# Turning the weights of the first 512 keys on the tensor engine in query blocks 8 to 15 of a forgetting-attention layer

## The chip, the cores and the metric

The kernel runs on one core of one Trainium2 chip. The metric is device time in microseconds (us), the median over runs. A core has TensorE (PE; its weight loads are listed as PEld), VectorE (DVE), ScalarE (ACT), GpSimd (POOL), a queue on SyncE (SP) that issues most DMAs, and 16 DMA engines. Each has its own list of instructions and goes through it in order.

## The reference

One layer, sequence 2048, width 1024, 16 heads of 64, all in float32: forgetting attention, then an MLP. `x` is (1, 2048, 1024).

```python
h = rms_norm(x, norm_mix) * (1 + sc_m) + sh_m
q, k, v, f_pre = split(h @ fox_w_in)
q = rms_norm(q, fox_q_norm); k = rms_norm(k, fox_k_norm)      # per head
F = cumsum(log_sigmoid(f_pre + fox_b_f))                      # per head, over time
logits = q @ k.T * 64 ** -0.5 + (F[t] - F[s])                 # only s <= t
x = x + g_m * ((softmax(logits) @ v) @ fox_w_out)
h = rms_norm(x, norm_mlp) * (1 + sc_f) + sh_f
x = x + g_f * (square(relu(h @ w_mlp_in)) @ w_mlp_out)
```

The shifts, scales and gates (`sc_m` and so on) come from `silu(c) @ w_ada + b_ada`.

## The kernel before

**Two halves.** Up to about 1500 us the kernel does the projections and the attention, from then on the output projection and the MLP. Products that need float32 accuracy are made from a high and a low part, three matmuls each (`mm3`, lines 132 to 134).

**Attention.** The 16 heads go in 8 pairs `g`; each pair goes through 16 query blocks `i` of 128 queries; each block through its two heads `h`. Block `i` sees `W = (i + 1) * 128` keys. For one (g, i, h):

- `att_scores`: TensorE makes the scores of up to 1024 keys into one of two PSUM tiles `S` (lines 537, 538; line 540 adds the mask); VectorE adds `F`, writes them to `L` (three buffers, float32, 2048 wide) and takes the maximum (line 544, line 549).
- `att_exp`: ScalarE does Exp in place on `L` (line 555) and then, in chunks of up to 1024 keys (`PW`), writes the weights times 32768 as f16 into the front half of a tile `ph` (line 562): the high part.
- `att_transpose`: VectorE writes the low part, `L * 32768 - high`, behind it (line 574). In the last pair, from block 8 on, GpSimd takes 256 columns of each chunk wider than 512 (lines 578, 579). Then the SP queue issues one DMA transpose of the chunk, both parts (line 582), into a tile `pT`, which holds keys on partitions. There are four `ph` and five `pT`.
- `att_values`: TensorE multiplies each turned block of 128 keys with the values, high part with high and low values side by side (line 600), low part with the high values (line 601), into `po`; after the second head VectorE and GpSimd finish the block (lines 608 to 611) and SP writes it to DRAM (line 613).

In the order of the code a head's scores come first, then the turning of the head before it, then its own Exp; the value products follow two to four heads later.

**Beside it** run the projections of the next head pair (`sweep`): `psq` matmuls (lines 487 to 489) on `hT` blocks that SP loads (`hl`, line 403) and ScalarE and GpSimd split (lines 406, 407); their results are normed, and q and k are turned by TensorE through `pqk` (lines 435, 445): four float32 transposes into one bank, read by ScalarE and VectorE (lines 437, 438, 447, 448). `pqk` sits in the pool `psT`, which has one bank:

```python
psT = st.enter_context(tc.tile_pool(name="psT", bufs=1, space=PSUM))
NL, NPH, NPT, NK, NV, NQD = 3, 4, 5, 6, 7, 1
AHEAD, LEAD, LAG_S, LAG_L = 1, 0.7, 3, 2
```

In the first pairs the rest of `w_ada` is read as well: `wa` tiles of 512 KB, summed on VectorE (lines 195, 197).

**Order.** The code interleaves attention and projections by shares of work done. A planner then fixes the order on each engine when the kernel is built: it goes by the order of the code and by its own estimates of when an operand and a buffer are ready, with score matmuls ahead (`PR_S = 100`, the other offsets are 0).

Of the kernel before, what the change touches and what calls it, by code (L numbers as in the profile page):

```python
# [14 lines left out]
F32 = mybir.dt.float32  # L15
# [3 lines left out]
AF = mybir.ActivationFunctionType  # L19
ALU = mybir.AluOpType  # L20
# [4 lines left out]
P = 128  # L25
# [4 lines left out]
HD = 64  # L30
KB = D // P
NT = S // P
TJ = 512
# [6 lines left out]
PSCALE = 32768.0  # L40
PW = 1024
# [4 lines left out]
PR_S, PR_T, PR_E, PR_PL, PR_PO, PR_OT = 100, 0, 0, 0, 0, 0  # L46
PR_Q, PR_QE, PR_SP, PR_SN, PR_AD, PR_DT = 0, 0, 0, 0, 0, 0
EPOOL, WOP = 0, 0
POOL_B, POOL_I, POOL_G = 2, 8, 7
NEARLY, EARLY0 = 5, 12  # L50
TAPER, LEAD1 = 6.6, 0.6
QSH, QDM = 0, 0
LEAD0, NORM_AT, ADA0, ADA1, NF = 0.5, 8, 60, 10, 5


# [2 lines left out]
def fox_layer(ctx, tc, x, c, norm_mix, norm_mlp, w_ada, b_ada, w_mlp_in, w_mlp_out,  # L58
              fox_w_in, fox_b_f, fox_q_norm, fox_k_norm, fox_w_out, out):
    nc = tc.nc  # L60
# [18 lines left out]
    ident = con.tile([P, P], F32, name="ident")  # L79
# [56 lines left out]
    def pri(n):  # L136
        return tc.high_priority(offset=n)
# [3 lines left out]
    blk = blk8[:RB]  # L141
# [25 lines left out]
    pt = psQ.tile([P, TJ], F32, tag="Q", name="ptrows")  # L167
# [7 lines left out]
    with ExitStack() as st:  # L175
        psS = st.enter_context(tc.tile_pool(name="psS", bufs=2, space=PSUM))
        psT = st.enter_context(tc.tile_pool(name="psT", bufs=1, space=PSUM))
# [4 lines left out]
        def big(nm):  # L182
# [4 lines left out]
                                       op0=ALU.mult, op1=ALU.mult)  # L187
# [334 lines left out]
        def att_scores(g, i, h, st, L):  # L522

            j, rb = divmod(i, RB)
            W = (i + 1) * P
            q, qz = qT[g, j]
            qs = slice(rb * P, (rb + 1) * P)
            mx = sb.tile([P, NJ // 2], F32, tag="mx", name=f"mx{g}_{i}_{h}", bufs=6)
            for cch in range(j + 1):
                w = min(TJ, W - cch * TJ)  # L530
                k = kT[g, cch]
# [16 lines left out]
            with pri(PR_T):  # L548
                nc.vector.tensor_reduce(out=st[:, h:h + 1], in_=mx[:, :j // 2 + 1], axis=AX.X, op=ALU.max, negate=True)  # L549

        def att_exp(g, i, h, st, L):

            W = (i + 1) * P
            with pri(PR_E):
                nc.scalar.activation(L[:, :W], L[:, :W], AF.Exp, bias=st[:, h:h + 1], scale=1.0,  # L555
                                     accum_out=st[:, 2 + h:3 + h])
            phs = []
            for s0 in range(0, W, PW):
                w = min(PW, W - s0)
                ph = sb.tile([P, 2 * PW], F16, tag="ph", name=f"ph{g}_{i}_{h}_{s0}", bufs=NPH)  # L560
                with pri(PR_E):
                    nc.scalar.activation(ph[:, :w], L[:, s0:s0 + w], AF.Copy, scale=PSCALE)  # L562
                phs.append(ph)
            return phs

        def att_transpose(g, i, h, L, phs):
            W = (i + 1) * P
            pts = []
            for n, ph in enumerate(phs):
                s0 = n * PW  # L570
                w = min(PW, W - s0)
                c = w - min(w, POOL_B * P) if i >= POOL_I and g >= POOL_G and w > TJ else w
                with pri(PR_PL):
                    nc.vector.scalar_tensor_tensor(ph[:, w:w + c], L[:, s0:s0 + c], PSCALE, ph[:, :c],  # L574
                                                   op0=ALU.mult, op1=ALU.subtract)
                    if c < w:
                        lt = L[:, s0 + c:s0 + w]
                        nc.gpsimd.tensor_scalar(lt, lt, PSCALE, None, op0=ALU.mult)
                        nc.gpsimd.tensor_tensor(ph[:, w + c:2 * w], lt, ph[:, c:w], op=ALU.subtract)
                pT = sb.tile([P, 2 * PW // P, P], F16, tag="pT", name=f"pT{g}_{i}_{h}_{s0}", bufs=NPT)  # L580
                with pri(PR_DT):
                    nc.sync.dma_start_transpose(pT[:, :2 * w // P, :], ph[:, :2 * w])
                pts.append(pT)
            return pts

        po_of, n_po = {}, [0]
        po_all = psO.tile([P, 2, 2, P], F32, tag="O", name="po")
# [1 line left out]
        def att_values(g, i, h, st, pts):  # L589
            nb = i + 1  # L590
            if h == 0:
                po_of[g, i] = po_all[:, n_po[0] % 2]
                n_po[0] += 1
            po = po_of[g, i]
            for b in range(nb):
                v = vT[g, b // RB][:, b % RB, h, :]
                pT, bb = pts[b * P // PW], b % (PW // P)
                nw = min(PW // P, nb - b + bb)
                with pri(PR_PO):
                    nc.tensor.matmul(po[:, h, :], lhsT=pT[:, bb, :], rhs=v, start=(b == 0), stop=False)  # L600
                    nc.tensor.matmul(po[:, h, 0:HD], lhsT=pT[:, nw + bb, :], rhs=v[:, 0:HD],
                                     start=False, stop=(b == nb - 1))
                if b % RB == RB - 1:
                    yield
            if h == 1:
                ot = sb.tile([P, 2, HD], F32, tag="ot", name=f"ot{g}_{i}", bufs=2)
                with pri(PR_OT):
                    nc.vector.reciprocal(st[:, 4:6], st[:, 2:4])
                    nc.vector.tensor_reduce(out=ot, in_=po.rearrange("p h (b d) -> p h d b", b=2), axis=AX.X,
                                            op=ALU.add)  # L610
                (nc.vector if g == NG - 1 else nc.gpsimd).tensor_tensor(
                    ot, ot, st[:, 4:6].unsqueeze(2).to_broadcast([P, 2, HD]), op=ALU.mult)
                nc.sync.dma_start(o_d[i][:, g * P:(g + 1) * P], ot.rearrange("p h d -> p (h d)"))
                del po_of[g, i]

        def attention():
            prev, late = None, []
            per = [C0 + 34.0 * (i + 1) for i in range(NT)]
            tot = 2.0 * sum(per)
            for g in range(NG):  # L620
                for i in range(NT):
                    st_ = sb.tile([P, 6], F32, tag="st", name=f"st{g}_{i}", bufs=6)
                    for h in range(2):
                        L = big(f"L{g}_{i}_{h}")
                        pv = iter(())
                        while len(late) > (LAG_S if i < 8 else LAG_L):
                            for _ in pv:
                                pass
                            pv = att_values(*late.pop(0))
                        nch = i // RB + 1  # L630
                        yield (g, i // RB), per[i] / tot / nch
                        for n, _ in enumerate(att_scores(g, i, h, st_, L)):
                            next(pv, None)
                            if n < nch - 1:
                                yield (g, i // RB), per[i] / tot / nch
                        if prev is not None:
                            late.append((*prev[:4], att_transpose(*prev[:3], *prev[4:])))
                        prev = (g, i, h, st_, L, att_exp(g, i, h, st_, L))
                        for _ in pv:
                            pass  # L640
            late.append((*prev[:4], att_transpose(*prev[:3], *prev[4:])))
            while late:
                for _ in att_values(*late.pop(0)):
                    pass
# [81 lines left out]
    psT = ctx.enter_context(tc.tile_pool(name="psT2", bufs=2, space=PSUM))  # L726
    sb = ctx.enter_context(tc.tile_pool(name="p2", bufs=2, reuse_waits="tile"))

    def ring(tag, shape, dt, nm):
        if tag == "w":  # L730
            return pw.tile(shape, dt, tag=tag, name=nm, bufs=8)
        return sb.tile(shape, dt, tag=tag, name=nm,
                       bufs={"raw": 4, "h": 8, "a": 8, "ya": 2, "s": 4, "g": 2}[tag])
# [97 lines left out]
    for r in range(2):  # L831
        g = ring("g", [P, D], F32, f"gate_bc{r}")
# [29 lines left out]
    def split(raw, nm):  # L862
        w = ring("w", [P, 2, D], F32R, nm)
        nc.scalar.copy(w[:, 0, :], raw)  # L864
        nc.vector.tensor_tensor(w[:, 1, :], raw, w[:, 0, :].bitcast(F32), op=ALU.subtract)  # L865
        return w

    for j in range(NJ):
        hT = load_hT(j) if j > 0 else h2_first
        ya = ring("ya", [P, RB, D], F32, f"ya{j}")  # L870
        for ch in range(NCH):
            aT, w2s = [], []
            for b in range(CB):
# [4 lines left out]
                w = split(wr, f"w1_{j}_{fb}")  # L878
# [68 lines left out]
```

## Time and profile before

| | |
|---|---|
| median of 3 runs | 3117.88 us (3115.86 to 3118.42) |
| the profiled execution | 3121.49 us, its span 3119.8 us |
| TensorE, weight loads, VectorE, ScalarE, GpSimd busy | 2870.4, 2375.9, 1930.7, 1433.1, 1040.5 us |
| DMA over the span | 502.34 MB, mean 161 GB/s |
| mean granted TensorE clock | 0.966 of 2.4 GHz |

The span goes from the first to the last instruction; busy times are unions over that span. A share of busy time is a mean over stages with different limits, so the rows below are taken by stage. "A <- B" in the rows on waits reads: A stood idle until B was done. Matmuls overlap, so their durations add up to more than the busy time. The clock column is the granted share of 2.4 GHz; the level below is 1.2 GHz.

### The profile page before, as it was taken

The numbers are of one execution on the slowest core, as the hardware profiler recorded it, in microseconds if no ns is written. First come the engines' busy times: TensorE is split into PE (matmuls) and PEld (weight loads), VectorE is DVE, ScalarE is ACT, GpSimd is POOL, SyncE is SP. The second block draws the span as 40 slices with busy tenths as digits, with TensorE's granted clock in tenths as the row PEclk, the third lists the DMA queues.
The fourth block names the chain that finished last, engine by engine and source line by source line (L and its number), as shares of the span: only waits on it lengthen the run. The fifth ranks groups of instructions, "written<-read, shape, count | busy, mean of one in ns | idle before, by whom it ended". The sixth has DMA issues, their size and how long they took to land.

```text
span 3119.8 us, 44614 instructions
## 1 busy us (share of the span) xinstructions
PE 2870.4 (92%) x16587; PEld 2375.9 (76%) x16587; DVE 1930.7 (62%) x3319; ACT 1433.1 (46%) x2267; POOL 1040.5 (33%) x811
## 2 busy tenths in 40 slices
PE   4788889888988898988999999999999999999999
PEld 4667777777877777776788888788887888878887
DVE  6688978988888877878356433443335333453334
ACT  4466766666676767766233322232222223222321
POOL 3354545545464645445332100410013001311103
PEclk9799989999999999998999999999999999999999
DMA  8479999999999989979755432543235323352332
GB/s 274 124 174 208 208 193 218 209 204 208 213 209 211 201 191 197 189 163 211 215 191 200 132 93 80 172 138 95 75 108 203 94 81 108 95 192 91 108 94 69
DMA packets 852122, 502.34 MB, mean 161 GB/s; under 512 B 585396, under 2 KB 782076, under 8 KB 851904
## 3 DMA queue, kind: packets, MB, share of 16 engines
q1 hardware_dynamic: 843536, 469.60, 62.1%
q0 software_dynamic: 8368, 29.89, 2.5%
q8 instruction: 130, 2.13, 0.3%
q14 instruction: 88, 0.72, 0.1%
HBM read 310.50 MB, written 46.28 MB: 114 GB/s over the span
## 4 chain that ended last, share of the span: by engine, by line
PE 49%; DVE 1%; DMA 1%; ACT 0%; issue 0%; SPq 0%; POOL 0%; DVEq 0%; ACTq 0%
PE my L134 8%; PE my L132 7%; PE my L133 7%; PE pu L134 7%; PE pu L132 7%; PE pu L133 7%; PE py L132 1%; PE py L133 1%; PE py L134 1%; DVE w L865 1%; DMA w1r<-in_w_mlp_in_dram 1%; PE xt L799 0%; PE e_py L132 0%; DMA pT<-ph 0%; PE e_py L134 0%; PE e_py L133 0%
## 5 line engine op out<-in xcount | busy, mean ns | idle before, releaser
L574 DVE SCALAR_TENSOR_TENSOR ph<-L,ph 128x1024 f16<-128x1024 f32 (+7 forms) x384 | 438.3, 1152 | 81.2 <-ACT ph L562 79.5
L887 POOL TENSOR_TENSOR rl<-rl 128x512 f32<-128x512 f32 x128 | 139.1, 1086 | 1024.6 <-ACT rl L886 1019.7
L864 ACT CAST w<-w1r 128x1024 fp32r<-128x1024 f32 x128 | 133.5, 1043 | 598.6 <-PE my L134 553.5
L132 PE MATMUL my<-w,a 128*128 128x512 f32 x1024 | 405.0, 396 | 0.1
L133 PE MATMUL my<-w,a 128*128 128x512 f32 x1024 | 402.9, 394 | 0.0
L134 PE MATMUL my<-w,a 128*128 128x512 f32 x1024 | 395.9, 396 | 2.9 <-DVE a L890 2.9
L562 ACT ACTIVATE ph<-L 128x1024 f16<-128x1024 f32 (+7 forms) x384 | 301.7, 804 | 177.4 <-DMA pT<-ph 152.6
L407 POOL TENSOR_TENSOR hl<-hl,hh 128x1024 fp32r<-128x1024 f32 x120 | 299.5, 2497 | 243.7 <-ACT hh L406 205.4
L487 PE MATMUL psq<-w,hh 128*128 128x384 f32 (+1 forms) x960 | 343.5, 359 | 26.5 <-DVE v L496 12.5
L489 PE MATMUL psq<-w,hl 128*128 128x384 f32 (+1 forms) x960 | 354.4, 371 | 3.2 <-POOL hl L407 2.9
L544 DVE CUSTOM_DVE_ANT_0 L<-S,F 128x1024 f32<-128x1024 f32 (+7 forms) x384 | 343.1, 904 | 19.5 <-PE S L538 6.7
L488 PE MATMUL psq<-w,hh 128*128 128x384 f32 (+1 forms) x960 | 342.7, 359 | 6.1 <-POOL w L333 6.1
L555 ACT ACTIVATE L<-L,st 128x128 f32<-128x128 f32 (+15 forms) x256 | 306.7, 1198 | 89.2 <-DVE st L549 84.9
L537 PE MATMUL S<-kT,qT 128*128 128x512 f32 (+3 forms) x640 | 261.8, 411 | 77.4 <-DVE mx L544 66.6
L600 PE MATMUL po<-v,pT 128*128 128x128 f16 x2176 | 277.1, 228 | 55.4 <-DMA pT<-ph 47.0
L865 DVE TENSOR_TENSOR w<-w1r,w 128x1024 fp32r<-128x1024 f32 x128 | 169.9, 1328 | 236.6 <-ACT w L864 236.6
L915 DVE TENSOR_TENSOR ya<-my,ya 128x512 f32<-128x512 f32 x192 | 128.0, 687 | 292.7 <-PE my L134 292.7
L134 PE MATMUL pu<-m_h,w 128*128 128x512 f32 x768 | 304.4, 396 | 0.0
L132 PE MATMUL pu<-m_h,w 128*128 128x512 f32 x768 | 303.8, 396 | 0.0
L133 PE MATMUL pu<-m_h,w 128*128 128x512 f32 x768 | 301.8, 393 | 0.0
L865 DVE TENSOR_TENSOR w<-w2r,w 128x1024 fp32r<-128x1024 f32 x128 | 165.7, 1295 | 203.7 <-ACT w L864 203.7
L600 PEld LDWEIGHTS <-pT 128*128 128x128 f16 x2176 | 205.1, 103 | 86.2 <-DMA pT<-ph 58.3
(214 smaller groups left out, 6115.8 us busy)
## 6 DMA issues: line engine op xcount, KB each, us to landing
w1r<-in_w_mlp_in_dram SPq DMA_DIRECT2D x128, 512.0 KB
w2r<-in_w_mlp_out_dram SPq DMA_DIRECT2D x128, 512.0 KB
hl<-hT_d SPq DMA_DIRECT2D x120, 512.0 KB
F<-nF_d SPq DMA_DIRECT2D x64, 256.0 KB
wa<-in_w_ada_dram SPq DMA_DIRECT2D x32, 512.0 KB
x<-in_x_dram SPq DMA_DIRECT2D x27, 512.0 KB
wr<-in_fox_w_in_dram SPq DMA_DIRECT2D x64, 192.0 KB
h_d<-h2r POOLq DMA_DIRECT2D x24, 512.0 KB, 3.4
```

Source lines behind the costliest of these rows:

```text
L132: nc.tensor.matmul(ps, lhsT=a[0], rhs=b[0], start=first, stop=False)
L133: nc.tensor.matmul(ps, lhsT=a[0], rhs=b[1], start=False, stop=False)
L134: nc.tensor.matmul(ps, lhsT=a[1], rhs=b[0], start=False, stop=last)
L487: nc.tensor.matmul(ps[:, :n], lhsT=hh, rhs=w[:, 0, :n], start=(kb == 0), stop=False)
L488: nc.tensor.matmul(ps[:, :n], lhsT=hh, rhs=w[:, 1, :n], start=False, stop=False)
L489: nc.tensor.matmul(ps[:, :n], lhsT=hl, rhs=w[:, 0, :n], start=False, stop=(kb == KB - 1))
L544: nc.vector.tensor_tensor_reduce(out=L[:, c0:c1], in0=s2[:, :c1 - c0], in1=Fb[g, h, cch // 2][:, :c1 - c0], scale=1.0, scalar=-3.0e38, op0 ...
L555: nc.scalar.activation(L[:, :W], L[:, :W], AF.Exp, bias=st[:, h:h + 1], scale=1.0, accum_out=st[:, 2 + h:3 + h])
L562: nc.scalar.activation(ph[:, :w], L[:, s0:s0 + w], AF.Copy, scale=PSCALE)
L574: nc.vector.scalar_tensor_tensor(ph[:, w:w + c], L[:, s0:s0 + c], PSCALE, ph[:, :c], op0=ALU.mult, op1=ALU.subtract)
L600: nc.tensor.matmul(po[:, h, :], lhsT=pT[:, bb, :], rhs=v, start=(b == 0), stop=False)
L865: nc.vector.tensor_tensor(w[:, 1, :], raw, w[:, 0, :].bitcast(F32), op=ALU.subtract)
```

## The change

For blocks 0 to 7 nothing changes. For blocks 8 to 15 the keys are divided otherwise: the first 512 keys ("pe"), then the rest in chunks of up to 1024 ("dma") as before. The "pe" part gets no `ph`: after Exp, TensorE turns four blocks of `L` in float32 into the bank of `psT` (a tile `pp`), ScalarE writes the high part from there into the first half of a `pT` buffer, VectorE the low part into its second half. `att_values` gets a list of (high, low) blocks instead of computing the places.

```diff
+TURN_I = 8
...
+        def plan(i):
+            W = (i + 1) * P
+            if i < TURN_I:
+                return [(s0, min(PW, W - s0), "dma") for s0 in range(0, W, PW)]
+            return [(0, TJ, "pe")] + [(s0, min(PW, W - s0), "dma") for s0 in range(TJ, W, PW)]
...
-            for s0 in range(0, W, PW):
-                w = min(PW, W - s0)
+            for s0, w, how in plan(i):
+                if how == "pe":
+                    phs.append(None)
+                    continue
                 ph = sb.tile([P, 2 * PW], F16, tag="ph", name=f"ph{g}_{i}_{h}_{s0}", bufs=NPH)
...
+            by_block = []
+            for (s0, w, how), ph in zip(plan(i), phs):
+                n = w // P
                 pT = sb.tile([P, 2 * PW // P, P], F16, tag="pT", name=f"pT{g}_{i}_{h}_{s0}", bufs=NPT)
+                if how == "pe":
+                    pt = psT.tile([P, TJ], F32, tag="T", name=f"pp{g}_{i}_{h}")
+                    for b in range(n):
+                        nc.tensor.transpose(pt[:, blk[b]], L[:, s0 + b * P:s0 + (b + 1) * P], ident)
+                    hi, lo = [pT[:, k * n:(k + 1) * n, :].rearrange("p b c -> p (b c)") for k in range(2)]
+                    nc.scalar.activation(hi, pt, AF.Copy, scale=PSCALE)
+                    nc.vector.scalar_tensor_tensor(lo, pt, PSCALE, hi, op0=ALU.mult, op1=ALU.subtract)
+                else:
...
+                    with pri(PR_DT):
+                        nc.sync.dma_start_transpose(pT[:, :2 * w // P, :], ph[:, :2 * w])
+                by_block += [(pT[:, b, :], pT[:, n + b, :]) for b in range(n)]
+            return by_block
...
-                    nc.tensor.matmul(po[:, h, :], lhsT=pT[:, bb, :], rhs=v, start=(b == 0), stop=False)
-                    nc.tensor.matmul(po[:, h, 0:HD], lhsT=pT[:, nw + bb, :], rhs=v[:, 0:HD],
+                    nc.tensor.matmul(po[:, h, :], lhsT=p_hi, rhs=v, start=(b == 0), stop=False)
+                    nc.tensor.matmul(po[:, h, 0:HD], lhsT=p_lo, rhs=v[:, 0:HD],
                                      start=False, stop=(b == nb - 1))
```

The branch after `else` holds the split of lines 574 to 579 unchanged, with the chunks of the new division.

## Rows read from the trace of the kernel before

**Rows 1.** Stages: us, busy us per engine, granted clock, DMA share, GB/s

```profile
212.00:1477.00 1265.00, 1099.85 (x8640) 941.28 (x8637) 1075.91 (x2112) 866.13 (x1438) 654.95 (x491) 0.94 0.98 202
1950.00:2340.00 390.00, 388.89 (x1666) 312.36 (x1665) 161.01 (x180) 108.39 (x140) 64.98 (x49) 1.00 0.37 117
```

**Rows 2.** Waits of TensorE, 212 to 1477 us: us in total, times, longest

```profile
PE S L537 <- DVE mx L544: 64.1, 50, 4.7
PE po L600 <- DMA pT<-ph: 37.4, 31, 3.1
PE pqk L435 <- POOL qn L429: 4.0, 3, 2.2
PE pqk L445 <- DVE qT L438: 2.8, 3, 1.3
```

**Rows 3.** Waits of ScalarE and VectorE, 212 to 1477 us

```profile
ACT ph L562 <- DMA pT<-ph: 147.0, 99, 6.4
DVE ph L574 <- ACT ph L562: 73.9, 74, 3.6
DVE acc L197 <- DMA wa<-in_w_ada_dram: 24.6, 17, 5.2
```

**Rows 4.** Waits of the SP queue, whole span

```profile
SPq L582 <- PE po L601: 141.4, 88, 5.5
```

**Rows 5.** Busy time in four stretches, columns as in the stages above

```profile
319.80:1010.00 690.20, 598.77 (x4654) 514.97 (x4653) 593.21 (x1122) 465.12 (x787) 357.68 (x258) 0.94 1.01 208
1010.00:1326.30 316.30, 281.92 (x2254) 242.45 (x2255) 261.40 (x528) 226.59 (x383) 168.53 (x126) 0.95 0.96 194
498.30:667.20 168.90, 143.60 (x1147) 126.93 (x1146) 147.63 (x280) 113.50 (x195) 90.79 (x64) 0.98 1.00 208
667.20:843.20 176.00, 151.86 (x1161) 129.26 (x1160) 153.37 (x285) 120.81 (x202) 89.74 (x65) 0.91 1.02 211
```

**Rows 6.** DMA traffic, 319.8 to 1010 us: the queue, then issues by size

```profile
q1 hardware_dynamic: 329281, 142.88, 100.1%
hl<-hT_d SPq DMA_DIRECT2D x65, 512.0 KB
wa<-in_w_ada_dram SPq DMA_DIRECT2D x30, 512.0 KB
F<-nF_d SPq DMA_DIRECT2D x33, 256.0 KB
wr<-in_fox_w_in_dram SPq DMA_DIRECT2D x32, 192.0 KB
o_d<-ot SPq DMA_DIRECT2D x64, 64.0 KB
```

**Rows 7.** Groups by form on ScalarE, 212 to 1477 us: busy, mean, idle

```profile
L562 ACT ACTIVATE ph<-L 128x1024 f16<-128x1024 f32 x154 | 161.8, 1055 | 74.5 <-DMA pT<-ph 71.2 <-DVE acc L197 1.9 <-issue 0.4
L562 ACT ACTIVATE ph<-L 128x512 f16<-128x512 f32 x30 | 18.6, 623 | 6.4 <-DMA pT<-ph 6.3
```

**Rows 8.** Groups by form on VectorE, 212 to 1477 us

```profile
L574 DVE SCALAR_TENSOR_TENSOR ph<-L,ph 128x1024 f16<-128x1024 f32 x140 | 207.3, 1484 | 36.3 <-ACT ph L562 35.3
L574 DVE SCALAR_TENSOR_TENSOR ph<-L,ph 128x128 f16<-128x128 f32 x30 | 19.1, 636 | 13.7 <-ACT ph L562 13.7
L438 DVE SCALAR_TENSOR_TENSOR qT<-pqk,qgain,qT 64x512 fp32r<-64x512 f32 x58 | 43.2, 746 | 3.5 <-ACT qT L437 2.6
```

**Rows 9.** Timeline of TensorE: start us, us, instruction

```profile
800.83 0.61 PE L445 MATMUL pqk<-ident,qn 128*128 128x128 f32 x4
801.20 0.42 PE L487 MATMUL psq<-w,hh 128*128 128x384 f32 x1
```

**Rows 10.** Line 767's transposes alone, 1529 to 1650 us: TensorE, weight loads, clock

```profile
1529.00:1650.00 121.00, 11.94 (x88) 10.21 (x88) 1.00 0.51 186
```

**Rows 11.** The first wait again, 319.8 to 1010 us, then 1010 to 1326

```profile
PE S L537 <- DVE mx L544: 34.2, 28, 3.9
PE S L537 <- DVE mx L544: 17.5, 11, 4.7
```

More of the change, by code (lines that the diff above doesn't have):

```diff
@@ L566, in att_transpose @@
         def att_transpose(g, i, h, L, phs):
[L567 to L579, printed above, removed]
-                pT = sb.tile([P, 2 * PW // P, P], F16, tag="pT", name=f"pT{g}_{i}_{h}_{s0}", bufs=NPT)
-                with pri(PR_DT):
-                    nc.sync.dma_start_transpose(pT[:, :2 * w // P, :], ph[:, :2 * w])
-                pts.append(pT)
@@ L584, in att_transpose @@
-            return pts
+            by_block = []
+            for (s0, w, how), ph in zip(plan(i), phs):
+                n = w // P
+                pT = sb.tile([P, 2 * PW // P, P], F16, tag="pT", name=f"pT{g}_{i}_{h}_{s0}", bufs=NPT)
+                if how == "pe":
[6 more added lines that the diff above has]
+                else:
+                    c = w - min(w, POOL_B * P) if i >= POOL_I and g >= POOL_G and w > TJ else w
+                    with pri(PR_PL):
+                        nc.vector.scalar_tensor_tensor(ph[:, w:w + c], L[:, s0:s0 + c], PSCALE, ph[:, :c],
+                                                       op0=ALU.mult, op1=ALU.subtract)
+                        if c < w:
+                            lt = L[:, s0 + c:s0 + w]
+                            nc.gpsimd.tensor_scalar(lt, lt, PSCALE, None, op0=ALU.mult)
+                            nc.gpsimd.tensor_tensor(ph[:, w + c:2 * w], lt, ph[:, c:w], op=ALU.subtract)
+                    with pri(PR_DT):
+                        nc.sync.dma_start_transpose(pT[:, :2 * w // P, :], ph[:, :2 * w])
+                by_block += [(pT[:, b, :], pT[:, n + b, :]) for b in range(n)]
@@ L596, in att_values @@
                 v = vT[g, b // RB][:, b % RB, h, :]
-                pT, bb = pts[b * P // PW], b % (PW // P)
-                nw = min(PW // P, nb - b + bb)
+                p_hi, p_lo = pts[b]
                 with pri(PR_PO):
-                    nc.tensor.matmul(po[:, h, :], lhsT=pT[:, bb, :], rhs=v, start=(b == 0), stop=False)
-                    nc.tensor.matmul(po[:, h, 0:HD], lhsT=pT[:, nw + bb, :], rhs=v[:, 0:HD],
+                    nc.tensor.matmul(po[:, h, :], lhsT=p_hi, rhs=v, start=(b == 0), stop=False)
+                    nc.tensor.matmul(po[:, h, 0:HD], lhsT=p_lo, rhs=v[:, 0:HD],
                                      start=False, stop=(b == nb - 1))
```

## The prediction

> **What bounds the kernel now.** I read the busy time by stage first, then who waits for whom in the stage that the change touches, then the DMA traffic there. In the stage table [rows 1] the reader should see two kinds of stage: in attention the DMA engines are full, in the MLP (1950 to 2340 us) they are busy 37%. The change lives in the first kind: from 212 us, where query block 8 of the first head pair is reached, to 1477 us, where the last head's maximum is taken, there are 1265 us. In them DMA is 98% busy, TensorE 1099.9 us (87%), VectorE 1075.9 (85%), ScalarE 866.1 (68%). Before 212 us no block above 7 is worked on, and after 1477 us only the last heads' turning and value products are left of the work that changes. So everything is won or lost in these 1265 us, 165 of which TensorE stands idle.
>
> What TensorE waits for [rows 2] is mostly two things: a score tile that VectorE hasn't read yet (64.1 us) and a turned weight tile from DMA (37.4). One step further back [rows 3] ScalarE waits 147.0 us for a ph buffer that DMA is still reading, and VectorE 73.9 us for that ScalarE cast. VectorE takes its instructions in order, so the score tiles behind the waiting split come late, and TensorE after them. Part of the 64.1 us is thus DMA too, though its row names VectorE. The SP queue stands 141.4 us in front of transposes whose pT buffer TensorE hasn't finished [rows 4]: the ring of five pT is short already.
>
> **What it removes.** 8 blocks x 2 heads x 8 pairs = 128 heads with 4 key blocks each: 512 of 2176 block transposes, 64 KB each (hi and lo, f16), 33.6 MB. What is that worth in DMA time? In 319.8 to 1010 us the hardware queue moved 142.9 MB [rows 6]. The copies listed there (hl 34.1 MB, wa 15.7, F 8.7, o_d 4.2, wr 6.3) come to 69.0; about 74 MB are transposes. The MLP stage moves 117 GB/s at a share of 0.37 [rows 1], 316 GB/s at full share. At that pace the copies take 218 of the 690 us, the transposes 472: some 156 GB/s, so 33.6 MB cost 215 us. At the stage's mean of 202 GB/s it would be 166. I take 215; the DMA share would fall from 0.98 to about 0.8. It also drops 64 issues on the SP queue: heads of blocks 8 to 11 now make one DMA transpose, 12 to 15 still two.
>
> The Trainium skill, "Advanced Engine Details and Errata", section "X-Bar Transpose (TRN2)", speaks against the change here: it says that such transposes run as fast as ordinary DMAs, at 350 to 400 GB/s. By that the 33.6 MB would free only an estimated 84 to 96 us. The rows above disagree: with DMA full, transposes and copies together reach 208 GB/s.
>
> **What it adds.** *TensorE*: 128 groups of four f32 transposes. The nearest row is the same operation on pqk: a group starts at 800.83 and the next matmul at 801.20 [rows 9], 0.37 us; the group alone lasts 0.61. I take 0.42, so **+54 us** (47 to 78). *ScalarE*: the hi cast reads PSUM instead of SBUF. The 512-column form takes 0.62, the 1024-column one 1.06 [rows 7], so 0.11 per 128 columns and 0.19 fixed. Blocks 8 to 11 issue as many casts as before, 12 to 15 one more: 64 x 0.19 = +12 us on an engine idle for 399 us; that idle time hides it. *VectorE*: the lo split from PSUM costs about 0.75, as the qT form does [rows 8]; a split from SBUF is 0.12 per 128 columns and 0.52 fixed (1.48 and 0.64). Blocks 8 to 11: 0.75 + 0.52 - 0.48 against 2 x 0.52, -0.25 x 64 = -16 us; blocks 12 to 15: +0.27 x 64 = +17. Together nothing. GpSimd's share in the last pair falls from 24 to 16 of its 256-column splits and VectorE takes these, about 2 us.
>
> **What it makes wait.** The four transposes need the exponentials of that head and the only bank of psT, which pqk uses too; it is free again when VectorE has written lo. Behind them in TensorE's queue stand value matmuls, projections and the next scores, and for those VectorE's maximum and ScalarE's Exp wait. On ScalarE the next Exp and the hh casts are queued behind hi, on VectorE the next score tile behind lo. Today some 58 such groups (8 pairs x 4 sweeps x 2, less six that come before 212 us) wait 4.0 + 2.8 us in this stage [rows 2], 0.12 us a group: 128 x 0.12 = **+15 us**. Below it could be 0. Above, a group that finds the bank just taken waits for the other group's 0.61, cast 0.62 and split 0.75: 2.0 us, 253 us for all. I take the row because it is the same bank and the same wait. The pT ring is loaded more: blocks 12 to 15 take three of its five buffers a head instead of two. A full ring costs SP 1.6 us a time now (141.4 over 88 waits [rows 4]); 64 heads make 102 us of waiting, on SP and ScalarE, which the idle time of ScalarE and the shorter DMA queue should cover. Without that cover some of it lands on TensorE, within the upper bound above.
>
> **What it gives back to TensorE.** The wait for pT (37.4 us) goes mostly, since DMA is no longer full: **-30** (0 to -37). Of VectorE's 189 us of idle time 98.5 are behind ph or behind wa loads [rows 3], 52%; the same part of 64.1 is **-33** (0 to -64). I don't take it all: in 1010 to 1326 us, with a DMA share of 0.96, the score wait is no smaller for a head pair than before 1010 us (17.5 us over two, 34.2 over four [rows 11]). The granted clock is 0.94, that is 12% of the time at 1.2 GHz. It is up and down between the pairs [rows 5]: 0.98 in 498 to 667 us with 143.6 us busy, 0.91 in the next with 151.9. With less idle time I expect 0.955, 1.5% of 1100: **-17** (0 to -44).
>
> **Sum by waits:** 54 + 15 - 30 - 33 - 17 = -11 us.
>
> **Sum by DMA.** The trace holds an experiment of its own [rows 5]: four head pairs in 319.8 to 1010 us with 30 wa loads [rows 6], two in 1010 to 1326.3 without. A pair takes 172.6 us with them, 158.2 without: -14.4. That is 3.9 MB less a pair, 12.4 us at 316 GB/s, though VectorE also drops its sums over wa there. If time follows DMA time fully, the change gives -215 + 54 + 15 = -146.
>
> The two lie far apart because waits name only the last in a chain, and because TensorE can't be filled. I stay nearer the first: -35. Then the stage lasts 1230 us with 1100 + 54 - 17 = 1137 busy, 92%; the pairs of [rows 5] have 85 to 89%, and at 100% it would be 1137, the floor (-128). So 3121.5 (the profiled execution: span 3119.8 and 1.7 around it) - 35 = 3086.5; the runs' median is 3.6 below the profiled one, so **3083 us**.
>
> **Rivals.**
> *A, the forecast* (0.60): DMA leaves the first place, TensorE at 90 to 95% takes it, -10 to -75: 3043 to 3108.
> *B, hidden* (0.15): the handshake of scores between TensorE and VectorE sets the pace, as its unmoved 8.6 and 8.8 us a pair would say [rows 11]. What is given back equals what is added: -10 to +10, 3108 to 3128.
> *C, the bank* (0.13): TensorE stands in front of psT. My -35 holds 15 us for it; at 0.12 + 35/128 = 0.39 us a group the gain is gone, at 1 us it is +78: 3196. For it: one bank, three readers in a row, used 24 times a pair instead of 8. Against it: the waits of today are small because other matmuls are put between.
> *D, the clock* (0.05): transposes don't hold the clock up and it drops to 0.91 as in 667 to 843 us, 3% of 1100 = +33 instead of -17: +15, 3133. Against it, in 1529 to 1650 us 88 such transposes run among matmuls at a granted 1.00 [rows 10].
> The Trainium skill, "TensorE: Matmul & The Clock Gate", section "Part 4: PE-mode transpose", is behind D: it says transposes don't count as work for the clock gate, and gives about 275 ns for one, an estimated 141 us for 512. By the rows it is 0.1 us each at pace, and the granted 1.00 doesn't agree with the rule.
> *E, all of DMA* (0.07): -75 to -128, 2990 to 3043.
>
> **Chances.** Anything under 0.2% (6 us) can't be told from no change. Faster: 0.56 of A, 0.04 of B, 0.01 of D, E: 0.68. Same: 0.04 + 0.07 + 0.01 = 0.12. Slower: 0.04 of B, C, 0.03 of D: 0.20. The range 3035 to 3128 takes in A, B and a little of E; left out are C, most of D and most of E, some 0.2. A's own range is 3043 to 3108.
>
> **What would show it.** Right: DMA share near 0.8 over the attention stage, ScalarE's wait for pT under half of 147 us, TensorE's wait for pT below 15, its busy share at 92%, new pp transposes at 0.1 us each. Wrong: TensorE idle in front of the pp transposes for more than 30 us, hi casts that wait for a pT buffer with Exp behind them, a DMA share that stays above 0.9, or a granted clock below 0.94.

## The result, and the profile after

The changed kernel takes **3311.93 us** (median of 4 runs, 3307.9 to 3312.45) against 3118.15 for the kernel before beside it: a ratio of 1.062, interval 1.0601 to 1.0638, or 194 us slower. The prediction was 3083, range 3035 to 3128. It was wrong in sign and by far. In the times below one execution is left out, of the kernel before with pqk in `psQ`: it took 6399.6 us, about twice the other three.

The stage from block 8 of the first pair to the last head's maximum, in the kernel after (columns as in [rows 1]: stretch, its us, busy us of TensorE, its weight loads, VectorE, ScalarE, GpSimd, granted clock, DMA share, GB/s):

```profile
210.00:1677.00 1467.00, 1198.57 (x9143) 1046.07 (x9144) 1037.98 (x2174) 881.04 (x1501) 624.60 (x483) 0.89 0.70 152
```

It is 202 us longer than the 1265 of [rows 1]; nothing else in the kernel moved by much. The DMA share fell from 0.98 to 0.70, that is from 1240 to 1027 us of DMA time in a longer stage, so the relief came. But no other engine took DMA's place: TensorE is at 82%, VectorE at 71%, ScalarE at 60%, all less than before. A stage in which every engine has become less busy waits in a chain. TensorE's 202 us more are 99 us more busy and 103 us more idle (268 instead of 165), and its waits name the place, here from 210 to 1672 us, against [rows 2]:

```profile
PE pp L585 <- DVE kT L449: 48.1, 15, 5.0
PE S L538 <- DVE mx L545: 46.0, 69, 2.9
PE pqk L446 <- DVE qT L439: 36.4, 10, 5.9
PE po L616 <- DMA pT<-ph: 33.5, 28, 4.9
PE po L616 <- ACT pT L587: 20.3, 28, 1.5
...
PE pp L585 <- DVE pT L588: 13.7, 12, 1.6
PE pp L585 <- DVE qT L439: 7.8, 3, 2.6
PE pp L585 <- DVE gate L223: 3.6, 2, 1.8
...
PE pp L585 <- DVE lw L232: 3.0, 6, 0.6
```

Six of these rows are TensorE in front of the one bank of `psT`, until VectorE has read the tile that was in it: 48.1 + 36.4 + 13.7 + 7.8 + 3.6 + 3.0 = 113 us. In [rows 2] the only such row is 2.8. Of the other engines' rows in [rows 3], ScalarE's wait for a `ph` buffer has fallen from 147.0 to 84.8 us and VectorE's wait for ScalarE's cast has grown from 73.9 to 140.4. Two rows are new, and both wait for the transposes themselves (the last two):

```profile
DVE ph L592 <- ACT ph L572: 140.4, 99, 6.2
ACT ph L572 <- DMA pT<-ph: 84.8, 60, 4.6
ACT pT L587 <- PE pp L585: 59.0, 57, 3.0
DVE L L545 <- PE pp L585: 51.1, 57, 3.8
```

In the last row VectorE can't write the next scores into `L`, because the transposes that read that buffer haven't run yet. The single operations cost what was expected:

```profile
L585 PE MATMUL pp<-ident,L x512: 270/273/477, 242.8 to 1697.9; 128*128 128x128 f32 x171
L587 ACT ACTIVATE pT<-pp x128: 571/597/617, 244.1 to 1698.7; 128x512 f16<-128x512 f32 x128
L588 DVE SCALAR_TENSOR_TENSOR pT<-pp,pT x128: 664/683/692, 245.2 to 1699.3; 128x512 f16<-128x512 f32 x128
```

The three times are minimum, median and maximum in ns: 0.60 us for hi (the high part) and 0.68 for lo (the low part), near the 0.62 and 0.75 of [rows 7, 8]. It isn't the work of the readers that is dear.

One episode of the kernel after, first TensorE's timeline, then VectorE's, then ScalarE's:

```profile
700.87 0.63 PE L585 MATMUL pp<-ident,L 128*128 128x128 f32 x4 [2.59 <-DVE qT L439]
705.92 0.87 PE L446 MATMUL pqk<-ident,qn 128*128 128x128 f32 x4
712.75 1.08 PE L585 MATMUL pp<-ident,L 128*128 128x128 f32 x4 [5.00 <-DVE kT L449]
```

```profile
703.43 0.69 DVE L588 SCALAR_TENSOR_TENSOR pT<-pp,pT 128x512 f16<-128x512 f32 x1
...
707.11 2.81 DVE L592 SCALAR_TENSOR_TENSOR ph<-L,ph 128x1024 f16<-128x1024 f32 x1 [0.92 <-ACT ph L572]
709.95 0.68 DVE L449 TENSOR_TENSOR kT<-pqk,kT 64x512 fp32r<-64x512 f32 x1
710.66 1.22 DVE L421 TENSOR_REDUCE ssq<-sq 128x16 f32<-128x1024 f32 x1
711.91 0.69 DVE L449 TENSOR_TENSOR kT<-pqk,kT 64x512 fp32r<-64x512 f32 x1
...
713.87 1.23 DVE L545 CUSTOM_DVE_ANT_0 L<-S,F 128x1024 f32<-128x1024 f32 x1 [0.36 <-PE pp L585]
```

```profile
706.98 0.56 ACT L448 CAST kT<-pqk 64x512 fp32r<-64x512 f32 x1
710.66 0.58 ACT L448 CAST kT<-pqk 64x512 fp32r<-64x512 f32 x1 [3.12 <-DVE kT L449]
```

Read it as the history of one bank. pp takes it at 700.87 and is done with when VectorE ends lo at 704.12. pqk takes it at 705.92. Its four readers alternate between ScalarE and VectorE, and the first on VectorE stands behind a split of 2.81 us; the last ends at 712.60. Only then can the next pp start, at 712.75: TensorE had been idle for 5.00 us, and VectorE's score tile waits for the transposes after that. The matmul work of pqk takes 0.87 us; it keeps the bank for 6.7.

That could be read before the change, nine microseconds behind the row [rows 9] that I took a price from. There pqk's group starts at 800.83. Its readers in the kernel before, ScalarE's and VectorE's timelines:

```profile
801.48 0.58 ACT L447 CAST kT<-pqk 64x512 fp32r<-64x512 f32 x1 [0.37 <-PE pqk L445]
...
806.51 0.58 ACT L447 CAST kT<-pqk 64x512 fp32r<-64x512 f32 x1
```

```profile
804.60 0.69 DVE L448 TENSOR_TENSOR kT<-pqk,kT 64x512 fp32r<-64x512 f32 x1
...
809.38 0.69 DVE L448 TENSOR_TENSOR kT<-pqk,kT 64x512 fp32r<-64x512 f32 x1
```

The bank was held from 800.83 to 810.07, 9.2 us for 0.61 us of matmuls; 9.2 is also the median of the 58 groups of this stage. Eight of these a pair are 74 us of some 165. It was nearly half taken before 16 more tenants a pair came. It isn't full in the kernel after either: summed over all groups of the trace, from the first matmul to the end of the last reader, pqk holds it for 434 us and pp for 547, about 980 in a stage of 1467. So the waits in front of it can't be put down to a bank without room.

### The profile page after: what moved, and what is told of

The parts are those of the page before. It is cut to its first block, busy times and chain, and to the rows that moved or that the text cites. A ratio compares the mean times of both kernels' runs of the same rounds, so it can differ in the third digit from the quotient of the medians.

```text
span 3310.3 us, 45731 instructions
## 1 busy us (share of the span) xinstructions
PE 2960.2 (89%) x17099; PEld 2473.5 (75%) x17099; DVE 1891.6 (57%) x3383; ACT 1447.7 (44%) x2331; POOL 1001.2 (30%) x795
## 4 chain that ended last, share of the span: by engine, by line
PE 50%; DVE 3%; DMA 3%; issue 1%; ACT 1%; POOL 0%; SPq 0%; DVEq 0%; ACTq 0%; POOLq 0%
PE my L135 7%; PE my L133 7%; PE my L134 7%; PE pu L135 6%; PE pu L133 6%; PE pu L134 6%; DMA pT<-ph 2%; PE py L134 1%; PE py L133 1%; PE py L135 1%; DVE w L881 1%; DMA w1r<-in_w_mlp_in_dram 1%; PE S L538 1%; PE psq L490 1%; PE psq L488 1%
## 5 line engine op out<-in xcount | busy, mean ns | idle before, releaser
L592 DVE SCALAR_TENSOR_TENSOR ph<-L,ph 128x1024 f16<-128x1024 f32 (+7 forms) x320 | 322.6, 1013 | 152.6 <-ACT ph L572 150.2
L488 PE MATMUL psq<-w,hh 128*128 128x384 f32 (+1 forms) x960 | 337.5, 354 | 24.3 <-DVE v L497 16.0
L490 PE MATMUL psq<-w,hl 128*128 128x384 f32 (+1 forms) x960 | 337.8, 354 | 0.6 <-POOL hl L408 0.6
L489 PE MATMUL psq<-w,hh 128*128 128x384 f32 (+1 forms) x960 | 333.3, 350 | 0.0
L616 PE MATMUL po<-v,pT 128*128 128x128 f16 x2176 | 262.8, 231 | 68.8 <-DMA pT<-ph 42.5
L538 PE MATMUL S<-kT,qT 128*128 128x512 f32 (+3 forms) x640 | 269.1, 426 | 51.8 <-DVE mx L545 48.4
L572 ACT ACTIVATE ph<-L 128x1024 f16<-128x1024 f32 (+7 forms) x320 | 238.6, 754 | 117.6 <-DMA pT<-ph 95.4
```

What stands on the lines that cost most here:

```text
L488: nc.tensor.matmul(ps[:, :n], lhsT=hh, rhs=w[:, 0, :n], start=(kb == 0), stop=False)
L489: nc.tensor.matmul(ps[:, :n], lhsT=hh, rhs=w[:, 1, :n], start=False, stop=False)
L490: nc.tensor.matmul(ps[:, :n], lhsT=hl, rhs=w[:, 0, :n], start=False, stop=(kb == KB - 1))
L538: nc.tensor.matmul(sp, lhsT=q[:, h, qs], rhs=k[:, h, :w], start=True, stop=False)
L616: nc.tensor.matmul(po[:, h, :], lhsT=p_hi, rhs=v, start=(b == 0), stop=False)
```

## The experiments

Every kernel was timed in rounds with the kernel before on the same chip (3112 to 3129 us in all of them); "against before" is the difference of the medians in one call, and two kernels of different calls are compared by these differences. Line numbers move by a few between kernels.

**What the relief is worth.** First 512 keys of blocks 8 to 15 cast and split into `ph` as before, but not turned; their value products read the next turned blocks.

```diff
-                if how == "pe":
-                    phs.append(None)
-                    continue
...
+                if how == "pe":
+                    nc.vector.scalar_tensor_tensor(ph[:, w:2 * w], L[:, s0:s0 + w], PSCALE, ph[:, :w],
+                                                   op0=ALU.mult, op1=ALU.subtract)
+                    continue
...
+            return by_block[:i + 1 - len(by_block)] + by_block if len(by_block) < i + 1 else by_block
```

> The change without its tensor-engine part: the first 512 keys of blocks 8 to 15 are cast and split into ph as before but not turned at all; their value products read the turned blocks of the keys that follow (that part of the result is left out). DMA relief alone. If DMA bounds the stage as the prediction had it, 35 to 130 us faster than before (2990 to 3083). If DMA was busy but not the bound, within 10 us of before (3108 to 3128).

Measured 3072.34, ratio 0.9854 (0.9837 to 0.987), -46 us. Its stage:

```profile
210.00:1431.00 1221.00, 1070.81 (x8627) 930.90 (x8625) 1087.90 (x2173) 873.24 (x1502) 641.42 (x479) 0.95 0.84 183
```

The DMA time is 0.84 x 1221 = 1026 us against 0.98 x 1265 = 1240: 214 us less (shares of two digits, so some 10 us either way), where the prediction had 215. The Trainium skill, "Advanced Engine Details and Errata", section "X-Bar Transpose (TRN2)", would have it at an estimated 84 to 96; this run doesn't agree. But 214 us of a full DMA are worth 46 us of time. And TensorE's two large waits, which the prediction wanted to shrink, are both a little longer than the 64.1 and 37.4 of [rows 2]:

```profile
PE S L538 <- DVE mx L545: 73.5, 65, 4.6
PE po L617 <- DMA pT<-ph: 39.8, 29, 6.4
```

Of the 44 us by which the stage is shorter, 29 are busy time of TensorE, at a granted clock of 0.95 instead of 0.94, and 15 are idle time from small rows.

**The transposes alone.** The same with the 512 transposes added and nothing reading them, in `psT` and then in `psQ`, the two banks of the projections.

```diff
                 if how == "pe":
+                    pt = psT.tile([P, TJ], F32, tag="T", name=f"pp{g}_{i}_{h}")
+                    for b in range(n):
+                        nc.tensor.transpose(pt[:, blk[b]], L[:, s0 + b * P:s0 + (b + 1) * P], ident)
```

> The first kernel of this call plus the 512 float32 transposes into the one bank of psT, which nothing reads; value products as in that kernel. If the transposes' own time is the cost, 54 to 85 us slower than the kernel without them. If the bank's readers are the cost, it stays within about 30 us of that kernel, so far under the changed kernel's 3312.

> The kernel with unread transposes (3216 in psT, 3072 without them), with them in psQ. If their cost in psT was waiting for pqk to leave the bank, what is left is TensorE's own time for them, 54 to 85 us: 3126 to 3157. If it was their place in TensorE's queue, about 3216 again.

In `psT` 3215.8 (1.0311, 1.0294 to 1.0328), +97 against before; in `psQ` 3134.45 (1.006, 1.0045 to 1.0075), +18. So with two banks the transposes cost 18 + 46 = 64 us (predicted 54, at most 78), and the same transposes cost another 80 in `psT`, without a single reader of their own: 143 in all, more than either of my two cases. The stage in `psQ`, then in `psT`:

```profile
210.00:1515.00 1305.00, 1154.03 (x9269) 995.93 (x9268) 1123.43 (x2182) 875.88 (x1505) 646.77 (x491) 0.96 0.81 173
```

```profile
210.00:1575.00 1365.00, 1148.67 (x9136) 1008.75 (x9137) 1081.01 (x2172) 876.07 (x1502) 637.20 (x477) 0.92 0.74 163
```

These 80 us are hardly time spent in front of the bank. What differs is TensorE's wait for turned weights, here in `psQ` and then, with the largest row in front of the bank, in `psT`:

```profile
PE po L620 <- DMA pT<-ph: 15.9, 13, 3.0
```

```profile
PE po L620 <- DMA pT<-ph: 73.9, 42, 6.7
...
PE pp L581 <- DVE kT L449: 6.3, 7, 2.2
```

The planner has made another order here. Counted in TensorE's order over blocks 8 to 15, the last value product of a block stands on average behind the scores of 4.5 later heads in `psQ` and of 3.0 in `psT` (4.7 in the kernel before), so it asks for its weights sooner. A new place for a tile is also a new order, and this pair of runs doesn't part the two.

The granted clock with the transposes in `psQ` is 0.96, higher than the 0.94 of [rows 1]. The Trainium skill, "TensorE: Matmul & The Clock Gate", section "Part 4: PE-mode transpose", says that transposes don't bring the clock to its upper level and don't count as busy in the same way. No loss of that kind is seen here, but the transposes are 86 of the 1154 us in which TensorE is busy, so this run doesn't decide it.

**The whole change with another place for pp.** In `psQ`, and in the ring of the scores:

```diff
-                    pt = psT.tile([P, TJ], F32, tag="T", name=f"pp{g}_{i}_{h}")
+                    pt = psQ.tile([P, TJ], F32, tag="Q", name=f"pp{g}_{i}_{h}")
```

> The changed kernel with the tile pp in the two banks of the projections (psQ) instead of the one bank of psT that it shares with pqk. If the shared single bank is the cause, 100 us or more of the 194 come back (under 3212). If the pT ring or the planner's order is, it stays above 3270.

> The changed kernel with pp in the ring of the scores (two tiles of two banks). If any second place cures it, 3120 to 3170. If taking a score tile's place is as bad as the single bank, because the next scores wait for VectorE's lo, above 3230.

In `psQ` 3132.31 (1.0045, 1.003 to 1.006): 180 of the 194 us come back with this one line, readers and all. Its stage:

```profile
210.00:1510.00 1300.00, 1151.75 (x9232) 998.40 (x9230) 1067.20 (x2180) 874.95 (x1502) 624.16 (x489) 0.96 0.81 173
```

That is 167 us less than in the kernel after: 120 us less idle time of TensorE, and 47 us less busy time for the same work at a granted clock of 0.96 instead of 0.89. TensorE's waits for VectorE in front of pp and pqk add up to 23 us, and those of the projections for a bank that held pp to 6, where the kernel after had 113 in front of `psT`.

In the score tiles 3190.39 (1.0225, 1.0208 to 1.0243): 120 us come back, between my two cases. There the value products stand behind 2.4 later heads and TensorE waits 97.4 us for turned weights.

The result in `psQ` is about that of the unread transposes, +14 and +18. Those still cast and split the same keys from SBUF, so this shows that hi and lo cost no more when they are read from the bank, as predicted.

**Other ways to unload the bank.** pqk moved to `psQ`, so that pp has `psT` for itself; pqk copied out by one ScalarE instruction (into a `ph` buffer), so that it leaves sooner; pp copied out likewise; both copied out.

```diff
-            pt = psT.tile([P, TJ], F32, tag="T", name=f"pqk{g}_{j}_0")
+            pt = psQ.tile([P, TJ], F32, tag="Q", name=f"pqk{g}_{j}_0")
```

```diff
+            pc = sb.tile([P, TJ], F32, tag="ph", name=f"pc{g}_{j}_0", bufs=NPH)
+            nc.scalar.copy(pc, pt)
+            pt = pc
```

```diff
+                    pf = sb.tile([P, TJ], F32, tag="ph", name=f"pf{g}_{i}_{h}", bufs=NPH)
+                    nc.scalar.activation(pf, pt, AF.Copy, scale=PSCALE)
+                    nc.scalar.copy(hi, pf)
+                    nc.vector.tensor_tensor(lo, pf, hi, op=ALU.subtract)
```

> The changed kernel with pqk moved to psQ instead, so that pp has the bank of psT for itself, still one. If the harm is that pp and pqk wait for each other's readers, 60 us or more come back (under 3250). If one bank is too few for pp by itself, or the cause is elsewhere, above 3270.

> The changed kernel, but ScalarE copies each pqk out of psT into a ph buffer and the four readers go to the copy, so that pqk leaves the bank after one read. In the trace of before, pqk keeps the bank some 10 us each time, 8 times a head pair (from its transposes to VectorE's last read), and pp in the changed kernel 4.0 us and 1.9 us until the next, 16 times: together about the length of a pair. If this occupancy of the one bank is the cause, 80 us or more of the 194 come back (under 3230). If not, the extra ScalarE work makes it 3310 or more.

> The changed kernel, but ScalarE copies pp out of psT in float32 and hi and lo are made from the copy, so that pp leaves the bank without VectorE. By occupancy pp's 4.0 us fall to about 2, 16 x 2 = 32 us a pair: 30 to 120 us come back (3190 to 3280). If the bank is not the cause: 3310 or more.

> Both copies. By occupancy the bank is then held about 8 x 2 + 16 x 2 = 48 us a pair, less than pqk alone holds it in the kernel before, so it should come to about the run with pp in psQ (3132), 3100 to 3160. If the bank is not the cause: above 3280.

3239.6 (1.0391, 1.0375 to 1.0407), 3264.77 (1.0479, 1.0464 to 1.0495), 3238.3 (1.0393, 1.0369 to 1.0417) and 3239.53 (1.0397, 1.0381 to 1.0412). Each brings back 46 to 73 us, in spite of the work that the copies add. That fits a cost of holding the bank, but every one of these kernels has a new order too. The copy of pqk brought back less than the 80 that I expected. With both copies, where I expected 3160 at most, no more came back than with one. The holds had not fallen as I had counted them: I expected some 48 us a pair, the trace has 283 us for pqk and 435 for pp, 90 a pair. The copies come late as well: they need a `ph` buffer, for which those of pp waited 16.3 us with both copies and 34.7 with pp's alone.

**What the move of pqk costs.** The kernel before with pqk in `psQ`, and the unread transposes with `psT` to themselves:

> The kernel before with pqk in psQ, nothing turned on the tensor engine. If the move of pqk into the projections' banks is costly by itself, 40 to 110 us slower than before (3158 to 3228), and the 3240 of the changed kernel with that move is mostly this. If the move is free, 3105 to 3130, and one bank is too few for pp alone.

> Transposes unread, in psT, with pqk in psQ: nobody else uses the bank for long and nobody reads it. If waiting for pqk to leave the bank was what the unread transposes paid in psT (3216 against 3134 in psQ), 3120 to 3150, plus what the move of pqk costs by itself. If not, about 3216.

3278.53 (1.0513, 1.0492 to 1.0534) and 3254.44 (1.0434, 1.0419 to 1.045). The move is dear by itself, 161 us. So the 3239.6 with pqk moved is not the price of pp in a single bank; against its own control it is 40 us faster. The unread transposes are 24 us faster than this control; if the relief is worth its 46 here too, which no run shows, they cost 22 with the bank to themselves. A tile with slow readers could do the same harm in the projections' banks, but the rows don't show that: TensorE doesn't wait for a bank so much as for turned weights (the control's first rows, 200 to 1700 us):

```profile
PE po L600 <- DMA pT<-ph: 136.1, 77, 6.5
PE S L537 <- DVE mx L544: 56.7, 42, 3.8
PE po L600 <- DVE ot L609: 36.9, 25, 3.2
```

Here too the order is another one: the value products stand behind 4.0 later heads instead of 4.7.

**Half of the blocks.** Only blocks 8 to 11 (two pT a head, as before), or 12 to 15 (three instead of two), with pp in `psQ`; then blocks 8 to 11 in `psT`.

```diff
-            if i < TURN_I:
+            if i < 8 or i >= 12:
```

> pp in psQ, and the turning on the tensor engine for blocks 8 to 11 alone (two pT a head, as before the change); 12 to 15 as before. If the ring of pT in blocks 12 to 15 is what eats the relief of the run with pp in psQ (3132), this is faster than before: 3085 to 3110. If each 64 heads cost as much as they relieve, 3115 to 3130.

> pp in psQ, and the turning on the tensor engine for blocks 12 to 15 alone, which then take three pT a head instead of two. If the ring of pT is the cost, slower than before: 3125 to 3160. If not, 3100 to 3125, like the other half.

> The changed kernel, pp in psT, but for blocks 8 to 11 alone: 8 uses of the bank a pair more instead of 16. The same with pp in psQ took 3103. By occupancy (pqk about 85 us a pair, 8 x 6 = 48 more, 133 of some 165) the bank has room: 3103 to 3145. If each use costs the same, half of 180 more: about 3193.

In `psQ` 3102.94 (0.9951, 0.9934 to 0.9967) and 3128.72 (1.0031, 1.002 to 1.0042): blocks 8 to 11 gain 16 us, 12 to 15 lose 9. In `psT` blocks 8 to 11 take 3230.58 (1.0361, 1.0344 to 1.0378): its place costs 130 us for 64 uses, and 180 for 128. I had expected at most 42 if occupancy alone counted, since there is room in the bank, or 90 if each use costs the same. It was more than both, though pqk and pp hold the bank for only 697 of the stage's 1383 us. TensorE stood only 21.6 us in front of it by its largest such row; the most it lost to value products whose weights weren't there (200 to 1700 us):

```profile
PE po L616 <- DMA pT<-ph: 99.1, 59, 7.0
PE S L538 <- DVE mx L545: 46.0, 49, 2.9
PE po L616 <- DVE ot L625: 23.6, 9, 6.1
PE pp L585 <- DVE kT L449: 21.6, 5, 5.0
```

**Order and pT ring.** The transposes moved ahead in the planner's order (`pri(100)` around them, in `psT`); and, in `psQ`, the pT ring divided into four for DMA and two of half size for pp, in the same memory (one load of `w_ada` at the start goes to another buffer for it).

```diff
-                    for b in range(n):
-                        nc.tensor.transpose(pt[:, blk[b]], L[:, s0 + b * P:s0 + (b + 1) * P], ident)
+                    with pri(100):
+                        for b in range(n):
+                            nc.tensor.transpose(pt[:, blk[b]], L[:, s0 + b * P:s0 + (b + 1) * P], ident)
```

```diff
+                    pT = sb.tile([P, 2 * RB, P], F16, tag="pP", name=f"pP{g}_{i}_{h}", bufs=2)
```

> The changed kernel, pp in psT, with the four transposes moved ahead in the planner's order by the same offset as the scores (100). In the changed kernel they come 17.8 us (median) after their head's Exp, so that a buffer of L is held 24 to 26 us; three buffers at 8 to 9 us a head. If the held L is how the bank costs time, the transposes come earlier, L is held under 20 us and 60 us or more come back (under 3250). If the bank alone sets the pace, they can't come earlier and it stays above 3290.

> pp in psQ, all of blocks 8 to 15, with the pT ring divided in the same memory: four buffers for DMA transposes, two of half size for the tensor engine's (one load of w_ada at the start goes to another buffer). If the shared ring holds the run with pp in psQ back, 20 us or more faster than its 3132 (under 3112). If not, 3125 to 3150, the four buffers costing a little.

3314.49 (1.0622, 1.0601 to 1.0644) and 3154.46 (1.0109, 1.0092 to 1.0126). Moving ahead changes nothing: the transposes start a median 17.9 us after their head's Exp, against 17.8 in the kernel after, so the offset didn't bring them forward. The divided ring is 21 us worse than the shared one, so dividing it doesn't help; whether five buffers are too few is not tested by it, and that blocks 12 to 15 lose remains without a shown cause.

**Is it just another order?** The kernel before with another lead of the projections:

```diff
-AHEAD, LEAD, LAG_S, LAG_L = 1, 0.7, 3, 2
+AHEAD, LEAD, LAG_S, LAG_L = 1, 0.66, 3, 2
```

> The kernel before with the lead of the projections 0.66 instead of 0.7: a new order, the same instructions. If a new order alone can cost 100 us, it shows here as more than 3150. If orders differ little as long as no bank is loaded more, 3105 to 3130.

3121.15 (1.0007, 0.9993 to 1.002). This new order of the same work costs nothing: its value products stand behind 4.6 later heads, where the kernel before has 4.7. It is one order, close to the old one in this respect. The kernels that place value products at 2.4 to 4.0 heads are not answered by it.

**A try for more.** Blocks 8 to 11 and, whole, blocks 0 to 3, in `psQ`:

> pp in psQ, blocks 8 to 11 as in the run that took 3103, and blocks 0 to 3 whole (no ph, no DMA transpose). It saves 64 small DMA transposes, 160 blocks, 10.5 MB, by the relief measured (46 us for 33.6 MB) 14 us, and costs 160 transposes on TensorE at 0.12, 19 us: 3100 to 3115. If their short latency helps the starts of the pairs, under 3095.

3135.52 (1.0054, 1.0037 to 1.0071), slower than blocks 8 to 11 alone, where I expected 3100 to 3115. The fastest kernel with the whole computation is the one that turns blocks 8 to 11 on TensorE through `psQ`: 0.5% faster than before and 6.3% faster than the change. Its runs spread from 3095 to 3116.

## Why the prediction was wrong

- **DMA time freed, 215 us: right** (214). **The relief's worth: too large.** The steps "-30", "-33" and "-17" together gave 80 us and the sum was then moved from -11 to -35 towards the sum by DMA. By itself the relief gave 46, and not by these steps: the wait for pT stayed (39.8 for 37.4) and the score wait grew (73.5 for 64.1). Only the lower busy time came, 29 us for the 17. With pp in `psQ` the wait for pT did fall, to 7.7, and the score wait again did not, 71.7. So "-33" was wrong in both. In the run with the relief alone the DMA share is 0.84 and TensorE is busy for 88% of the stage: DMA was full, but it was not the one bound. The score handshake (rival B) stayed.
- **TensorE's time, +54: a little small** (64). hi and lo at nothing: nothing speaks against it.
- **The bank, +15: the step that failed.** It measured 180 (changed kernel against pp in `psQ`). I took 0.12 us a group from the waits of 58 groups in a bank that was held for nearly half of the time and asked for only 8 times a pair, and multiplied by 128. Of the 6.8 us in that price 4.0 weren't even a wait for the bank, but for the normed q from GpSimd. And a wait at low load doesn't give the wait when there are three times as many tenants. The warning stood in the readers' timelines: 9.2 us of holding for 0.61 us of matmuls. The bound of 2.0 us a group that stands beside it in the prediction counted bare durations and left out the readers' queues, yet measured per group the cost is 1.4 us, within it. The prediction's rival C named this mechanism, put the point of decision at 0.39 us a group, and gave it 0.13.
- **The clock: wrong way.** Expected 0.955, it fell to 0.89, and was 0.96 where the same transposes didn't stand in front of the bank. In four of the stages above it was lower where TensorE stood idle for longer: 0.96 with 148 us idle (pp in `psQ`), 0.94 with 165 (before), 0.92 with 216 (unread, `psT`), 0.89 with 268 (after). So rival D, that transposes as such pull it down, isn't needed. The 88 transposes of [rows 10] were weak evidence on that: they are 11.94 of 121 us. Of TensorE's 99 us more busy time 52 are there with pp in `psQ` too; the other 47 go with the lower level.
- With the bank out of the way the change measured +14 (pp in `psQ`; +18 with unread transposes, which is the 64 less the 46). So the forecast of -35 would have missed without the bank too: the trade is DMA time that was worth a fifth of its length (46 of 214) for TensorE time worth most of its length (64 of the 86 us in which it is busy with them).

**What stays open.** That the place of pp costs the 180 us is shown by the run that changes nothing else in the code. In the kernel after, TensorE's waits in front of the bank make 113 us, against 29 for pp's banks with pp in `psQ`: 84 of the 120 us of idle time. The lower clock goes with the other 47 us of the stage. How much of this is the bank and how much the order that the planner made for it isn't separated. In the neighbours the loss isn't a wait for the bank: with unread transposes in `psT`, with pp in the score tiles and with pqk of the kernel before in `psQ` the value products stand 0.7 to 2.4 heads earlier than in the nearest kernel with the other place, and wait 74 to 136 us for DMA's transposes. That the planner's order is the cause there is likely and not tested; a run with one order and two places would show it. With half of the blocks in `psT` the value products stand at 4.6 heads, as in the kernel before, and still wait 99.1 us; why is open.

## What to carry to other kernels

Before something is put into a PSUM bank, read how long its present tenants keep it, from their first matmul to the end of the last reader's instruction in its queue, and multiply by their number; waits in front of it say little while it is half empty. This warns of a price and doesn't give it: by such sums I expected at most 42 us for half of the blocks and 3160 with both copies, and measured 130 and 3239.53. Where a planner makes the order from the places, look afterwards at how many heads lie between scores and value products. The Trainium skill says, "Perfetto Trace Analysis", section "Optimizing Tensor Performance", that independent groups should rotate through different banks, so that the reading of one overlaps the matmuls of the next. One line that does so gave back 180 us here; the same done to pqk in the kernel before cost 161. And a DMA that is busy all the time is worth only what a run without its transfers shows: here a fifth.

## What the runs showed of the hardware

Leaving out 33.6 MB of DMA transposes of f16 from SBUF to SBUF freed 214 us of the time of all 16 DMA engines: about 157 GB/s, as the prediction's 156, which rests on copies at the pace of the MLP stage (316 GB/s). 512 float32 transposes of 128x128 on TensorE, written to the two banks of `psQ` and unread, cost 64 us of the kernel's time, 0.125 us each, though a single one lasts 0.27 us.
